# Row-wise softmax of a batched diagonal: half batches in row-by-row dot products against whole batches in wide products and sums

## The chip, the cores and the metric

The kernel runs on one core of a Trainium2 chip. The metric is the device time of one execution in microseconds (us), the median of several runs. Profiled executions give the details; their own time stands beside their span, which is the time from the first to the last of the program's instructions.

The engines that matter here are VectorE (DVE in the profile), which does the dot products, ScalarE (ACT), which does the exponentials and issues the output transfers, GpSimd (POOL), which reduces across partitions, and SyncE (SP), which only issues the input transfers. 16 DMA engines move the data.

## The reference

`x` and `y` are float32 of shape (8, 4096, 512). Of the product of x and the transposed y only the diagonal is needed, so each of the 8 x 4096 outputs begins as the dot product of one row of x with the same row of y:

```python
gram = np.matmul(x, y.transpose(0, 2, 1))
diag = np.diagonal(gram, axis1=1, axis2=2)
diag = diag - diag.max(axis=-1, keepdims=True)
exp = np.exp(diag)
return (exp / exp.sum(axis=-1, keepdims=True)).astype(np.float32)
```

The softmax runs over the 4096 values of a batch. Each input is read once, 134.22 MB in all; the output has 0.13 MB.

## The kernel before

A batch has 4096 rows. They are laid over 128 partitions, so that partition p holds rows 32p to 32p + 31, which is one run of 64 KB in memory. A batch is worked on in two halves of 16 rows to a partition (`H = 16`).

The loop at L82 goes over batches and halves. For each half, `load` (L38) takes a new x tile and a new y tile from a pool with three buffers for each, and issues one transfer for each of the two on SP's queue, 4 MB apiece, in which each partition gets one run of 32 KB (L43, L44). The last half of the last batch is cut into pieces of 8, 4, 2, 1 and 1 rows. A load into a buffer that was used before waits until the dot products that read it are done; that wait stands on SP, and the transfers behind it on SP wait too.

`dots` (L48) then runs one VectorE instruction for each of the 16 rows (L51): it multiplies 512 elements of x and y, writes the products over x, and leaves their sum in one column of `diag`. The sum comes out of an accumulator, which shows in the profile as a second instruction, a read of the accumulator.

After the second half, `softmax` (L61) takes the maximum of the 32 columns (L65), the maximum over the partitions on GpSimd (L67), its negative (L69), the exponentials with their sums on ScalarE (L71), the sum over the partitions on GpSimd (L76), the reciprocal (L78) and the scaling (L79), and sends 128 runs of 128 bytes to the output from ScalarE's queue (L80).

The framework puts the semaphores for all this. Transfers from SP and ScalarE share eight completion semaphores in turn, so a transfer also waits until the transfer that had its semaphore before has landed.

Of the kernel before, what the change touches and what calls it, by code (L numbers as in the profile page):

```python
# [1 line left out]

# [5 lines left out]


@with_exitstack
def kernel(
    ctx: ExitStack,
    tc: tile.TileContext,
    x: bass.AP,
    y: bass.AP,
    out: bass.AP,
):
    nc = tc.nc
    f32 = mybir.dt.float32  # L20
    B, N, D = x.shape
    P = nc.NUM_PARTITIONS
    R = N // P
    H = R // 2


    xv = x.rearrange("b (p r) d -> b p r d", p=P)
    yv = y.rearrange("b (p r) d -> b p r d", p=P)
    ov = out.rearrange("b (p r) -> b p r", p=P)

    io = ctx.enter_context(tc.tile_pool(name="io", bufs=3))
    persist = ctx.enter_context(tc.tile_pool(name="persist", bufs=1))
    sm = ctx.enter_context(tc.tile_pool(name="sm", bufs=2))

    diag = persist.tile([P, B * R], f32, name="diag")
    res = persist.tile([P, B * R], f32, name="res")

    def load(b, r0, parts):  # L38
        xt = io.tile([P, H, D], f32, tag="xt", name="xt")
        yt = io.tile([P, H, D], f32, tag="yt", name="yt")  # L40
        o = 0
        for n in parts:
            nc.sync.dma_start(out=xt[:, o : o + n, :], in_=xv[b, :, r0 + o : r0 + o + n, :])  # L43
            nc.sync.dma_start(out=yt[:, o : o + n, :], in_=yv[b, :, r0 + o : r0 + o + n, :])  # L44
            o += n
        return xt, yt

    def dots(b, r0, xt, yt):  # L48
        for k in range(H):
            c = b * R + r0 + k  # L50
            nc.vector.scalar_tensor_tensor(  # L51
                out=xt[:, k, :],
                in0=xt[:, k, :],
                scalar=1.0,
                in1=yt[:, k, :],
                op0=mybir.AluOpType.mult,
                op1=mybir.AluOpType.mult,
                accum_out=diag[:, c : c + 1],
            )

    def softmax(b):  # L61
        db = diag[:, b * R : (b + 1) * R]
        rb = res[:, b * R : (b + 1) * R]
        mxp = sm.tile([P, 1], f32, tag="mxp", name="mxp")
        nc.vector.tensor_reduce(out=mxp, in_=db, axis=mybir.AxisListType.X, op=mybir.AluOpType.max)  # L65
        mx = sm.tile([P, 1], f32, tag="mx", name="mx")
        nc.gpsimd.partition_all_reduce(out_ap=mx, in_ap=mxp, channels=P, reduce_op=bass_isa.ReduceOp.max)  # L67
        nmx = sm.tile([P, 1], f32, tag="nmx", name="nmx")
        nc.vector.tensor_single_scalar(out=nmx, in_=mx, scalar=-1.0, op=mybir.AluOpType.mult)  # L69
        sump = sm.tile([P, 1], f32, tag="sump", name="sump")  # L70
        nc.scalar.activation(  # L71
            out=rb, in_=db, func=mybir.ActivationFunctionType.Exp,
            bias=nmx, scale=1.0, accum_out=sump,
        )
        ssum = sm.tile([P, 1], f32, tag="ssum", name="ssum")
        nc.gpsimd.partition_all_reduce(out_ap=ssum, in_ap=sump, channels=P, reduce_op=bass_isa.ReduceOp.add)  # L76
        rc = sm.tile([P, 1], f32, tag="rc", name="rc")
        nc.vector.reciprocal(out=rc, in_=ssum)  # L78
        nc.vector.tensor_single_scalar(out=rb, in_=rb, scalar=rc, op=mybir.AluOpType.mult)  # L79
        nc.scalar.dma_start(out=ov[b], in_=rb)  # L80

    for b in range(B):  # L82
        for h in range(2):
            last = b == B - 1 and h == 1
            parts = [8, 4, 2, 1, 1] if last else [H]
            xt, yt = load(b, h * H, parts)
            dots(b, h * H, xt, yt)
        softmax(b)


# [1 line left out]
_INS = ['x', 'y']  # L92
_OUTS = [((8, 4096), 'float32')]


# [23 lines left out]
```

## Time and profile before

| | before |
|---|---|
| median of 10 runs | 325.54 us (325.39 to 325.71) |
| the profiled execution's own time | 325.62 us |
| its span | 323.8 us |
| VectorE busy | 164.3 us, 544 instructions |
| ScalarE busy, GpSimd busy | 4.6 us, 6.1 us |
| input transfers (queue q1) | 5760 packets, 134.22 MB, 96.6% of 16 engines' time |
| output transfers (queue q10) | 1152 packets, 0.13 MB, 0.3% |
| mean rate of all transfers over the span | 415 GB/s |

Busy time is the time in which an engine has an instruction under way; issuing a transfer and waiting do not count. The share of a DMA queue is the time that its packets took, over the span of 16 engines. In the groups of instructions, the time after the bar is the busy time and the mean of one instruction in nanoseconds, then the time that the engine was idle just before, and what ended that. Instruction counts of the profile leave out waits. Since the instructions of one row overlap, a row takes less time than one instruction lasts: 16 rows take 9.90 us in the chain of waits, 0.62 us a row, where the instruction lasts 687 ns.

### The profile page before, as it was taken

The numbers are of one execution on the slowest core, as the hardware profiler recorded it, in microseconds if no ns is written. First come the engines' busy times: TensorE is split into PE (matmuls) and PEld (weight loads), VectorE is DVE, ScalarE is ACT, GpSimd is POOL, SyncE is SP. The second block draws the span as 40 slices with busy tenths as digits, with TensorE's granted clock in tenths as the row PEclk, the third lists the DMA queues.
The fourth block names the chain that finished last, engine by engine and source line by source line (L and its number), as shares of the span: only waits on it lengthen the run. The fifth ranks groups of instructions, "written<-read, shape, count | busy, mean of one in ns | idle before, by whom it ended". The sixth has DMA issues, their size and how long they took to land.

```text
span 323.8 us, 727 instructions
## 1 busy us (share of the span) xinstructions
DVE 164.3 (51%) x544; ACT 4.6 (1%) x17; POOL 6.1 (2%) x20
## 2 busy tenths in 40 slices
DVE  0029084290944709256191742908348091571994
ACT  1000000000000000000000000000000000000000
POOL 0000000000000000000000000000000000000000
DMA  8999999999999999999999999999999999999980
GB/s 324 453 405 437 453 426 413 455 421 421 453 429 415 454 421 418 454 419 425 453 421 421 456 413 429 449 414 434 449 413 433 450 403 441 449 409 427 417 313 10
DMA packets 6917, 134.39 MB, mean 415 GB/s; under 512 B 1792, under 2 KB 1792, under 8 KB 2560
## 3 DMA queue, kind: packets, MB, share of 16 engines
q1 hardware_dynamic: 5760, 134.22, 96.6%
q10 hardware_dynamic: 1152, 0.13, 0.3%
q14 instruction: 5, 0.04, 0.0%
HBM read 134.22 MB, written 0.13 MB: 415 GB/s over the span
## 4 chain that ended last, share of the span: by engine, by line
DMA 82%; DVE 16%; issue 1%; SPq 0%; POOLq 0%; POOL 0%; DVEq 0%
DMA yt<-in_y_dram 82%; DVE xt L51 16%; SPq L43 0%; DVE mxp L65 0%; POOLq L114 0%; POOL mx L67 0%; DVE res L79 0%; DVE rc L78 0%; DVEq L51 0%; DVEq L79 0%; POOLq L67 0%
## 5 line engine op out<-in xcount | busy, mean ns | idle before, releaser
L51 DVE SCALAR_TENSOR_TENSOR xt<-xt,yt 128x512 f32<-128x512 f32 x256 | 158.2, 687 | 144.2 <-DMA yt<-in_y_dram 144.1
L51 DVE DVE_READ_ACCUMULATOR xt<-xt,yt 128x1 f32 x256 | 21.1, 82 | 0.0
L67 POOL PARTITION_ALL_REDUCE mx<-mxp x8 | 2.8, 350 | 308.9 <-DVE mxp L65 308.9
L71 ACT ACTIVATE res<-diag,nmx 128x32 f32<-128x32 f32 x8 | 2.6, 321 | 315.2 <-DVE nmx L69 315.2
L78 DVE RECIPROCAL rc<-ssum 128x1 f32<-128x1 f32 x8 | 1.3, 164 | 7.6 <-POOL ssum L76 7.6
L69 DVE TENSOR_SCALAR nmx<-mx 128x1 f32<-128x1 f32 x8 | 1.2, 154 | 4.3 <-POOL mx L67 4.3
L76 POOL PARTITION_ALL_REDUCE ssum<-sump x8 | 3.1, 383 | 5.8 <-ACT res L71 5.8
L79 DVE TENSOR_SCALAR res<-res,rc 128x32 f32<-128x32 f32 x8 | 1.9, 241 | 0.9
L65 DVE TENSOR_REDUCE mxp<-diag 128x1 f32<-128x32 f32 x8 | 1.5, 186 | 0.3
L71 ACT ACTIVATION_READ_ACCUMULATOR res<-diag,nmx 128x1 f32 x8 | 1.5, 187 | 0.0
L71 ACT ACT_TABLE_LOAD x1 | 1.3, 1283 | 0.7 <-PEq L103 0.7
L103 POOL MEMSET const-float32-0.0<- 128x1 f32 x1 | 0.1, 98 | 0.2 <-issue 0.2
L103 POOL MEMSET const-bfloat16-1.0<- 128x1 bf16 x1 | 0.1, 102 | 0.0
L103 POOL MEMSET const-uint8-127<- 128x1 uint8 x1 | 0.1, 101 | 0.0
L103 POOL MEMSET const-float32-1.0<- 128x1 f32 x1 | 0.1, 98 | 0.0
## 6 DMA issues: line engine op xcount, KB each, us to landing
xt<-in_x_dram SPq DMA_DIRECT2D x15, 4096.0 KB, 39.6
yt<-in_y_dram SPq DMA_DIRECT2D x15, 4096.0 KB, 48.9
xt<-in_x_dram SPq DMA_DIRECT2D x1, 2048.0 KB, 34.8
yt<-in_y_dram SPq DMA_DIRECT2D x1, 2048.0 KB, 39.3
xt<-in_x_dram SPq DMA_DIRECT2D x1, 1024.0 KB, 41.3
yt<-in_y_dram SPq DMA_DIRECT2D x1, 1024.0 KB, 43.3
xt<-in_x_dram SPq DMA_DIRECT2D x1, 512.0 KB, 35.5
yt<-in_y_dram SPq DMA_DIRECT2D x1, 512.0 KB, 27.0
```

The source lines that it names most:

```text
L51: nc.vector.scalar_tensor_tensor(out=xt[:, k, :], in0=xt[:, k, :], scalar=1.0, in1=yt[:, k, :], op0=mybir.AluOpType.mult, op1=mybir.AluOpT ...
L65: nc.vector.tensor_reduce(out=mxp, in_=db, axis=mybir.AxisListType.X, op=mybir.AluOpType.max)
L67: nc.gpsimd.partition_all_reduce(out_ap=mx, in_ap=mxp, channels=P, reduce_op=bass_isa.ReduceOp.max)
L69: nc.vector.tensor_single_scalar(out=nmx, in_=mx, scalar=-1.0, op=mybir.AluOpType.mult)
L71: nc.scalar.activation(out=rb, in_=db, func=mybir.ActivationFunctionType.Exp, bias=nmx, scale=1.0, accum_out=sump,)
L76: nc.gpsimd.partition_all_reduce(out_ap=ssum, in_ap=sump, channels=P, reduce_op=bass_isa.ReduceOp.add)
L78: nc.vector.reciprocal(out=rc, in_=ssum)
L79: nc.vector.tensor_single_scalar(out=rb, in_=rb, scalar=rc, op=mybir.AluOpType.mult)
L103: nc = _bacc.Bacc("TRN2", target_bir_lowering=False, num_devices=1)
```

## The change

The kernel is laid out anew, with the order of its instructions as written.

There are now two whole x tiles, `xs0` and `xs1`, used in turn, and a single y tile, `ys`. Each has 32 rows to a partition, 64 KB.

Batches 0 to 5 are loaded with one transfer for x and one for y, each of 8 MB. One VectorE instruction multiplies all 32 rows, 16384 elements to a partition, over x (`dots_wide`), and a second one sums them in 32 groups of 512 (`sums_wide`). The next load into `ys` waits for the product; the next load into the same x tile waits for the sums.

Batch 6 is loaded with one transfer for x and two halves for y, and its dot products run row by row as before. Batch 7 comes in pieces of 8, 8, 8, 4, 2, 1 and 1 rows, also row by row. Each of its y pieces goes into `ys` and so waits for those rows of batch 6 that lie there.

The softmax runs in three groups. Batches 0 to 4 are done together (`group_exp` after the sums of batch 4, `group_out` between the product and the sums of batch 5); batches 5 and 6 together, with `group_exp` before row 2 of batch 7 and `group_out` before its row 10; batch 7 alone, by the same instructions as before (`last_softmax`). In the groups, the negative and the scaling are on ScalarE, and each group has one output transfer, with runs of 128 bytes.

```diff
-    io = ctx.enter_context(tc.tile_pool(name="io", bufs=3))
...
+    ctx.enter_context(tc.manual_schedule())
...
+    xs = [big.tile([P, R, D], f32, name=f"xs{i}") for i in range(2)]
+    ys = big.tile([P, R, D], f32, name="ys")
...
+    def load_x(b, r0, n):
+        nc.sync.dma_start(out=xs[b % 2][:, r0 : r0 + n, :], in_=xv[b, :, r0 : r0 + n, :])
+
+    def load_y(b, r0, n):
+        nc.sync.dma_start(out=ys[:, r0 : r0 + n, :], in_=yv[b, :, r0 : r0 + n, :])
+
+    def dots_wide(b):
+        xt = xs[b % 2]
+        nc.vector.tensor_tensor(out=xt, in0=xt, in1=ys, op=Alu.mult)
+
+    def sums_wide(b):
+        nc.vector.tensor_reduce(out=diag[:, b, :], in_=xs[b % 2], axis=X, op=Alu.add)
+
+    def dot_row(b, r):
+        xt = xs[b % 2]
+        nc.vector.scalar_tensor_tensor(
+            out=xt[:, r, :],
+            in0=xt[:, r, :],
+            scalar=1.0,
+            in1=ys[:, r, :],
+            op0=Alu.mult,
+            op1=Alu.mult,
+            accum_out=diag[:, b, r : r + 1],
+        )
+
+    def group_exp(name, b0, n):
...
+        nc.vector.tensor_reduce(out=mxp, in_=diag[:, b0 : b0 + n, :], axis=X, op=Alu.max)
+        nc.gpsimd.partition_all_reduce(out_ap=mx, in_ap=mxp, channels=P, reduce_op=bass_isa.ReduceOp.max)
+        nc.scalar.mul(nmx, mx, -1.0)
+        for i in range(n):
+            nc.scalar.activation(
+                out=res[:, b0 + i, :], in_=diag[:, b0 + i, :], func=Act.Exp,
+                bias=nmx[:, i : i + 1], scale=1.0, accum_out=sump[:, i : i + 1],
             )
+        nc.gpsimd.partition_all_reduce(out_ap=ssum, in_ap=sump, channels=P, reduce_op=bass_isa.ReduceOp.add)
+        return ssum
...
+    def group_out(name, b0, n, ssum):
+        rc = column(name + "rc", n)
+        nc.vector.reciprocal(out=rc, in_=ssum)
+        for i in range(n):
+            rb = res[:, b0 + i, :]
+            nc.scalar.activation(out=rb, in_=rb, func=Act.Copy, scale=rc[:, i : i + 1])
+        nc.scalar.dma_start(out=ov[:, b0 : b0 + n, :], in_=res[:, b0 : b0 + n, :])
...
-    for b in range(B):
-        for h in range(2):
-            last = b == B - 1 and h == 1
-            parts = [8, 4, 2, 1, 1] if last else [H]
-            xt, yt = load(b, h * H, parts)
-            dots(b, h * H, xt, yt)
-        softmax(b)
+    for b in range(wide):
+        load_x(b, 0, R)
+        load_y(b, 0, R)
+        dots_wide(b)
+        if b == wide - 1:
+            group_out("a", 0, wide - 1, first)
+        sums_wide(b)
+        if b == wide - 2:
+            first = group_exp("a", 0, wide - 1)
+
+    b = B - 2
+    load_x(b, 0, R)
+    for r0 in (0, R // 2):
+        load_y(b, r0, R // 2)
+        for r in range(r0, r0 + R // 2):
+            dot_row(b, r)
+
+    b = B - 1
+    r0 = 0
+    for n in (8, 8, 8, 4, 2, 1, 1):
+        load_x(b, r0, n)
+        load_y(b, r0, n)
+        for r in range(r0, r0 + n):
+            if r == 2:
+                second = group_exp("b", B - 3, 2)
+            if r == 10:
+                group_out("b", B - 3, 2, second)
+            dot_row(b, r)
+        r0 += n
+    last_softmax(b)
```

Here `B` is 8, `R` is 32 and `wide` is 6.

More of the change, by code (lines that the diff above doesn't have):

```diff
@@ L19 @@
     nc = tc.nc
+    ctx.enter_context(tc.manual_schedule())
     f32 = mybir.dt.float32
+    Alu = mybir.AluOpType
+    Act = mybir.ActivationFunctionType
+    X = mybir.AxisListType.X
     B, N, D = x.shape
@@ L23 @@
     R = N // P
-    H = R // 2
+    wide = B - 2
     xv = x.rearrange("b (p r) d -> b p r d", p=P)
     yv = y.rearrange("b (p r) d -> b p r d", p=P)
-    ov = out.rearrange("b (p r) -> b p r", p=P)
-    io = ctx.enter_context(tc.tile_pool(name="io", bufs=3))
[L32 to L58, printed above, removed]
-            )
@@ L61, in softmax @@
[L61 to L75, printed above, removed]
+    ov = out.rearrange("b (p r) -> p b r", p=P)
@@ new lines, with column @@
+    big = ctx.enter_context(tc.tile_pool(name="big", bufs=1))
+    small = ctx.enter_context(tc.tile_pool(name="small", bufs=1))
+    xs = [big.tile([P, R, D], f32, name=f"xs{i}") for i in range(2)]
+    ys = big.tile([P, R, D], f32, name="ys")
+    diag = small.tile([P, B, R], f32, name="diag")
+    res = small.tile([P, B, R], f32, name="res")
+    def column(name, n):
+        return small.tile([P, n], f32, name=name)
+    def load_x(b, r0, n):
+        nc.sync.dma_start(out=xs[b % 2][:, r0 : r0 + n, :], in_=xv[b, :, r0 : r0 + n, :])
@@ new lines, in group_exp @@
+    def group_exp(name, b0, n):
+        mxp, mx, nmx, sump, ssum = (column(name + s, n) for s in ("mxp", "mx", "nmx", "sump", "ssum"))
+        nc.vector.tensor_reduce(out=mxp, in_=diag[:, b0 : b0 + n, :], axis=X, op=Alu.max)
[5 more added lines that the diff above has]
+                bias=nmx[:, i : i + 1], scale=1.0, accum_out=sump[:, i : i + 1],
+            )
+        nc.gpsimd.partition_all_reduce(out_ap=ssum, in_ap=sump, channels=P, reduce_op=bass_isa.ReduceOp.add)
+        return ssum
@@ new lines, in group_out, with last_softmax @@
+    def group_out(name, b0, n, ssum):
[5 more added lines that the diff above has]
+        nc.scalar.dma_start(out=ov[:, b0 : b0 + n, :], in_=res[:, b0 : b0 + n, :])
+    def last_softmax(b):
+        db, rb = diag[:, b, :], res[:, b, :]
+        mxp, mx, nmx, sump, ssum, rc = (column("l" + s, 1) for s in ("mxp", "mx", "nmx", "sump", "ssum", "rc"))
+        nc.vector.tensor_reduce(out=mxp, in_=db, axis=X, op=Alu.max)
+        nc.gpsimd.partition_all_reduce(out_ap=mx, in_ap=mxp, channels=P, reduce_op=bass_isa.ReduceOp.max)
+        nc.vector.tensor_single_scalar(out=nmx, in_=mx, scalar=-1.0, op=Alu.mult)
+        nc.scalar.activation(out=rb, in_=db, func=Act.Exp, bias=nmx, scale=1.0, accum_out=sump)
@@ L76, in softmax @@
         nc.gpsimd.partition_all_reduce(out_ap=ssum, in_ap=sump, channels=P, reduce_op=bass_isa.ReduceOp.add)
-        rc = sm.tile([P, 1], f32, tag="rc", name="rc")
         nc.vector.reciprocal(out=rc, in_=ssum)
-        nc.vector.tensor_single_scalar(out=rb, in_=rb, scalar=rc, op=mybir.AluOpType.mult)
-        nc.scalar.dma_start(out=ov[b], in_=rb)
-    for b in range(B):
-        for h in range(2):
-            last = b == B - 1 and h == 1
-            parts = [8, 4, 2, 1, 1] if last else [H]
-            xt, yt = load(b, h * H, parts)
-            dots(b, h * H, xt, yt)
-        softmax(b)
+        nc.vector.tensor_single_scalar(out=rb, in_=rb, scalar=rc, op=Alu.mult)
@@ new lines, in last_softmax @@
+        nc.scalar.dma_start(out=ov[:, b, :], in_=rb)
+    for b in range(wide):
[14 more added lines that the diff above has]
+    b = B - 1
```

## The prediction

> **What bounds the kernel now.** I read the table of DMA queues first, then the chain that ended last, then a table of stretches, then the timeline at both ends. The columns of the queue table are packets, MB, and the share of 16 DMA engines' time.
>
> ```profile
> DVE 164.3 (51%) x544; ACT 4.6 (1%) x17; POOL 6.1 (2%) x20
> q1 hardware_dynamic: 5760, 134.22, 96.6%
> q14 instruction: 5, 0.04, 0.0%
> by line: DMA yt<-in_y_dram 81.9%; DVE xt L51 15.5%; issue 0.6%; SPq L43 0.5%; DVE mxp L65 0.2%; POOLq L114 0.1%; POOL mx L67 0.1%; DVE res L79 0.1%; DVE rc L78 0.1%; DVEq L51 0.0%; DVEq L79 0.0%; POOLq L67 0.0%
> L51 DVE SCALAR_TENSOR_TENSOR xt<-xt,yt 128x512 f32<-128x512 f32 x256 | 158.2, 687 | 144.2 <-DMA yt<-in_y_dram 144.1
> SPq L43 <- DVE xt L51: 133.0, 7, 19.7
> ```
>
> VectorE works half the time and idles 144 us, nearly all of it for y. SP waits up to 19.7 us for free buffers (last line), so its queue is always fed. The loads set the time, and VectorE's share in the chain is only that releases pass through it. The stretches (length, busy VectorE, ScalarE, GpSimd, clock, DMA share, GB/s) tell more:
>
> ```profile
> 22.47:61.20 38.73, 20.52 (x68) 0.41 (x2) 0.73 (x2) 1.00 1.00 433
> 303.40:314.60 11.20, 11.20 (x39) 0.00 (x0) 0.00 (x0) 1.00 0.94 377
> 314.60:318.40 3.80, 3.23 (x11) 0.00 (x0) 0.00 (x0) 1.00 0.06 22
> 318.40:323.80 5.40, 1.45 (x6) 0.41 (x2) 0.73 (x2) 1.00 0.03 5
> ```
>
> The first row is the full rate, 433 GB/s. The third is the surprise: for 3.8 us the DMA share is 0.06, one engine of sixteen. Fifteen engines are done by 314.6 and one works alone until 318.4. The last row is the tail, softmax and output, 5.4 us.
>
> The trace's packet records say why one engine is late. At 47.4, 124.9, 185.5 and 263.0 us an 8,192-byte packet of the instruction queue (q14) takes 0.31 to 0.33 us, and the 32 KB packet that starts just after it takes 1.87 us against 1.21: together 0.97 us lost each time. In the landing times of the 16 engines, the last lags the fifteenth by 0.1 us before the first fetch, then by 0.9, 1.8, 2.9 and 3.9. When the fetches start, VectorE has begun 53, 191, 306 and 444 instructions (waits included), about 130 apart; no other engine runs so many. I conclude that they are VectorE's instruction stream, and that the last 3.9 us of the load stage are these four fetches.
>
> **What the Trainium skill says.** (1) "Runtime: NRT & Kernel Launch", section Instruction fetch mechanics: the sequencer fetches its instructions by its own DMA queue, 256 in a 16 KiB block, thus 64 bytes each. The trace agrees in kind, its block is 8 KiB, which is 128 instructions and close to the 130 above. (2) "DMA: Bandwidth & Descriptors", section Where 436 GB/s comes from: a ceiling of 435 GB/s; the 433 here is nearly that, so transfers in bulk can gain very little. (3) "VectorE: DVE Perf Modes", section on the TRN2 errata: an fp32 product of two tensors takes (N+151)/0.96 ns. For N = 512 that is 691, the row above has 687. (4) The same page's perf-mode tier table has tensor_reduce at one element a cycle; the trace's 128x32 reduce at 186 ns fits 32 cycles with that fixed part.
>
> **The change, part by part.** The model is per DMA engine, and I check it on the kernel before. A packet of 16 KB takes 611 ns and one of 32 KB 1213, so a packet costs 9 ns beside its bytes.
>
> *Packets.* Each transfer has 128 runs, 8 on an engine, and one completion packet of 9 ns. Before: 40 transfers, 320 packets an engine. After: 12 whole-batch loads, x and two halves of y for batch 6, and 14 pieces of batch 7 make 29 transfers, 232 packets. Gain: 88 x 9 + 11 x 9 ns = 0.9 us. No trace shows a 64 KB run. If it is cut in two, the wide part has 104 packets more and the gain is gone (bounds 0 and 0.9 us). I take one packet.
>
> *Instruction fetches.* VectorE's 544 counted instructions become 148: 6 products, 6 sums, 2 group maxima and 2 reciprocals, 64 rows with 64 accumulator reads, 4 in the last softmax; with waits some 166 to 170. The first fetch came at the 53rd, the next at the 191st. So one fetch is left, at about row 12 to 15 of batch 6, near 278 us. Three of four go: 3 x 0.97 = 2.9 us off the late engine. Bounds: none left, 3.9; none removed, 0. I take 2.9.
>
> *The wide products and the new wait.* The product of 32 rows has N = 16384: 17.22 us as an estimate from (3). Below it stands 16384/0.96 = 17.07, above it 32 rows at their pace of 0.613 us, 19.6. There is one ys, so the issue of y(b+1) on SP waits for the product of batch b, and x(b+2) and all later loads stand behind it. Meanwhile x(b+1) flows. How long does a queue take to restart? At the start of the span:
>
> ```profile
> 0.72 0.36 SPq L43 DMA_DIRECT2D xt<-in_x_dram  x1
> 1.13 21.33 DMA yt<-in_y_dram
> ```
>
> x is issued at 0.72 and y, two transfers of 9.71 us later, has landed at 22.46, so 2.3 us are latency on idle engines. The loop from y to y is 0.09 (landing to VectorE) + 17.22 + 0.03 (to SP) + 2.3 + 19.35 (the y load at one packet per 64 KB) = 39.0 us; the loads of a batch alone are 38.7. So the gap g at each of y1 to y5 and the first half of y6 is at most 0.3 us at the cold latency. It is less if the reads of y overlap the end of x: the descriptors arrive 1.0 us after the issue (first packet at 1.72), and x has then 1.0 us to go. The last output shows a short way too, 1.4 us from issue to landing. I take g = 0.05, 6 x 0.05 = 0.3 us; bounds 0 and 2.0.
>
> *Sums.* x(b+2) waits for the sums of b: 17.2 + 17.2 after y(b) landed, issue 34.5 after it, and the queue is full until 38.7. Cover 4.2 us less a latency of 2.3; each us beyond that costs 5 us in all. Nothing charged. The first group's maximum (0.2) and the reciprocal sit in the same slack.
>
> *Rows of batches 6 and 7.* The sums of batch 5 end near 269.3; the 32 rows of batch 6 end at 289. Pieces of y7 wait for the rows of batch 6 in ys: rows 0 to 7 are done at 274.3, while y6 lands until 273.4 and the first x7 piece covers until 278.3. Later pieces have 5 us or more. VectorE has caught up before piece three (lands near 302.8), so the last row starts at its landing, as before.
>
> *Outputs.* The second group's output takes up the completion semaphore that the first group's output used, and the last x piece is the next user, so its issue on SP waits for that output. Output packets alternate with load packets on each engine (before, 8 of them took 13.5 us beside 32 KB packets). 40 packets of the first group from 254.8 pass by about 289; the second output is issued near 296.5 and its 16 pass by 306. The last x piece must be out by 309.5. Cover 3.5 us, nothing charged; beyond that every us costs one.
>
> *Tail.* The last softmax has the same instructions: 5.48 us from the last landing (318.36) to the span's end.
>
> Sum: the fifteenth engine's last landing, 314.63, less 0.9 = 313.7; one fetch +0.97 = 314.7; gaps +0.3 = 315.0; tail +5.48 = 320.5 span. The profiled execution took 325.62 with a span of 323.84, 1.78 around it: 322.3. The median is 0.08 below that execution: **322.2 us**.
>
> **Rivals.** *The gap opens* (slower). If product and latency together are longer than 19.2 (19.35 less the 0.12 of handing over), each batch adds the excess as g. At 321.9 without gaps, g = 0.7 brings it beyond 326.2, so it decides at product plus latency of 19.9. With the row pace as the product, 19.6, and the cold latency, g = 2.7 and 16 us are lost: 338. I price it half way, g = 1.35: 330. For it: one buffer for y and only 1 us between arrival of descriptors and dry queues. Against it: the formula fits the 687 ns row. *The late engine stays late* (no change): the fetches are not VectorE's, or another delay takes the engine; only packets are gained, 322.2 + 2.9 = 325.1. For it: the fetches are unevenly spaced (138, 115, 138 instructions). *Small gain*: g = 0.3 six times and 64 KB runs cut in two, 322.2 + 1.7 + 0.9 = 324.8. *Larger gain*: no fetch at all and no gap, 320.9.
>
> **How the numbers follow.** Main case 0.67, with the larger gain 0.70 (320.9 to 324); small gain 0.07; no change 0.10; slower 0.13. A change under about 0.2% (0.65 us) cannot be told from none. Faster 0.77, same 0.10, slower 0.13. The range, 320.9 to 325.3, leaves out the slower case and little more.
>
> **What would show it.** Right: y(b) landings 38.7 to 39.0 us apart; one q14 packet besides the start's and the end's, after 240 us; one engine alone for about 1 us at the end instead of 3.8; products near 17.2 us; q1 with 29 x 144 = 4,176 packets. Wrong: products over 18 us, a DMA share clearly under 1.00 at the end of each x, SP waiting for the second output, or again four fetches.

## The result: 332.6 us, 2.1% slower

| | before | after |
|---|---|---|
| median | 325.59 us (31 runs, 325.39 to 325.75) | 332.6 us (9 runs, 330.35 to 333.79) |
| ratio to before | | 1.0208 (95% interval 1.0195 to 1.0221) |
| profiled execution, its span | 325.62, 323.8 us | 332.23, 330.5 us |
| last landing of an input | 318.36 us | 325.01 us |
| last landing to the span's end | 5.48 us | 5.44 us |

The forecast was 322.2 us. The runs after also scatter by 3.4 us, where those of before scatter by 0.4.

These are the engine lines, the DMA queues and the groups of the page of the kernel after:

```profile
DVE 247.6 (75%) x148; ACT 6.2 (2%) x26; POOL 3.3 (1%) x10
q1 hardware_dynamic: 4176, 134.22, 95.6%
q14 instruction: 1, 0.01, 0.0%
DMA 58%; DVE 39%; issue 2%; SPq 0%; POOLq 0%; ACT 0%; POOL 0%; DVEq 0%; ACTq 0%
L55 DVE TENSOR_TENSOR xs<-xs,ys 128x16384 f32<-128x16384 f32 x6 | 103.3, 17225 | 71.6 <-DMA ys<-in_y_dram 71.6
L58 DVE TENSOR_REDUCE diag<-xs 128x32 f32<-128x16384 f32 x6 | 103.3, 17220 | 0.2
```

The counts are as forecast: 148 VectorE instructions, 4,176 packets, a single fetch of instructions (at 286.5 us in the packet records), products of 17.2 us. But VectorE's share of the chain has gone from 16% to 39%: the product is now a link between one load of y and the next. This is the chain in order of time (start, length, what):

```profile
1.14 40.91 DMA ys<-in_y_dram
...
42.16 17.24 DVE xs L55
59.39 0.02 issue
59.41 23.72 DMA ys<-in_y_dram
...
83.22 17.24 DVE xs L55
100.46 0.02 issue
100.48 22.23 DMA ys<-in_y_dram
...
140.05 23.61 DMA ys<-in_y_dram
...
181.01 23.88 DMA ys<-in_y_dram
...
222.24 21.98 DMA ys<-in_y_dram
```

Each y row runs from its issue to its landing. The data of one such load takes 19.35 us (8 packets of 2.418 us on each engine), so 4.4, 2.9, 4.3, 4.5 and 2.6 us go by beside the data. For 2.0 to 2.2 us of that the load stands behind the end of x, and nothing is lost; the rest is a hole. The landings of y are therefore 41.1, 39.6, 41.0, 41.2 and 39.3 us apart, against the 38.7 us that the bytes of a batch need.

In the stretches (length, busy VectorE, ScalarE, GpSimd, clock, DMA share, GB/s) the hole is directly visible behind the first such issue:

```profile
42.06:59.41 17.35, 17.23 (x1) 0.00 (x0) 0.00 (x0) 1.00 0.98 423
59.41:63.00 3.59, 3.58 (x1) 0.00 (x0) 0.00 (x0) 1.00 0.89 292
42.06:244.22 202.16, 172.55 (x11) 1.84 (x11) 0.84 (x2) 1.00 0.98 415
275.14:322.00 46.86, 40.37 (x122) 1.45 (x7) 1.53 (x2) 1.00 1.00 421
```

A packet counts with its bytes where it starts, so a short stretch shows a rate only roughly; the long third one is solid: 415 GB/s instead of 433. In the fourth, where y comes in small pieces and several transfers are always queued, the DMA share is 1.00 again. The packet records give the detail. After the issue at 59.41 the engines end x between 60.5 and 61.1. Most start y between 60.8 and 61.3, but two only at 61.97 and 62.69. The first y packet takes 2.9 to 3.65 us instead of 2.42, as the first packets at the start of the kernel do (2.6 to 3.5).

### The profile page after: what moved, and what is told of

It is laid out like the page before. It is cut to its first block, busy times and chain, and to the rows that moved or that the text cites. A ratio compares the mean times of both kernels' runs of the same rounds, so it can differ in the third digit from the quotient of the medians.

```text
span 330.5 us, 298 instructions
## 1 busy us (share of the span) xinstructions
DVE 247.6 (75%) x148; ACT 6.2 (2%) x26; POOL 3.3 (1%) x10
## 3 DMA queue, kind: packets, MB, share of 16 engines
q1 hardware_dynamic: 4176, 134.22, 95.6%
## 4 chain that ended last, share of the span: by engine, by line
DMA 58%; DVE 39%; issue 2%; SPq 0%; POOLq 0%; ACT 0%; POOL 0%; DVEq 0%; ACTq 0%
DMA ys<-in_y_dram 54%; DVE xs L55 31%; DVE diag L58 4%; DVE xs L62 4%; DMA out_dram<-res 3%; SPq L48 0%; POOLq L161 0%; ACT res L91 0%; POOL lmx L98 0%; DVE res L103 0%; DVE lmxp L97 0%; DVE lrc L102 0%; DVEq L55 0%; DVE arc L88 0%; DVE brc L88 0%
## 5 line engine op out<-in xcount | busy, mean ns | idle before, releaser
L55 DVE TENSOR_TENSOR xs<-xs,ys 128x16384 f32<-128x16384 f32 x6 | 103.3, 17225 | 71.6 <-DMA ys<-in_y_dram 71.6
L58 DVE TENSOR_REDUCE diag<-xs 128x32 f32<-128x16384 f32 x6 | 103.3, 17220 | 0.2
L62 DVE SCALAR_TENSOR_TENSOR xs<-xs,ys 128x512 f32<-128x512 f32 x64 | 39.8, 689 | 7.2 <-DMA ys<-in_y_dram 7.1
L62 DVE DVE_READ_ACCUMULATOR xs<-xs,ys 128x1 f32 x64 | 5.4, 84 | 0.0
L79 ACT ACTIVATE res<-diag,anmx 128x32 f32<-128x32 f32 x5 | 1.5, 308 | 0.0
L91 ACT ACTIVATE res<-res,arc 128x32 f32<-128x32 f32 x5 | 1.2, 309 | 19.5 <-DVE arc L88 19.5
L76 POOL PARTITION_ALL_REDUCE bmx<-bmxp x1 | 0.7, 735 | 57.1 <-DVE bmxp L75 57.1
L79 ACT ACTIVATION_READ_ACCUMULATOR res<-diag,anmx 128x1 f32 x5 | 0.9, 187 | 0.0
L83 POOL PARTITION_ALL_REDUCE bssum<-bsump x1 | 0.8, 800 | 1.1 <-ACT res L79 1.1
```

What stands on the lines that cost most here:

```text
L55: nc.vector.tensor_tensor(out=xt, in0=xt, in1=ys, op=Alu.mult)
L58: nc.vector.tensor_reduce(out=diag[:, b, :], in_=xs[b % 2], axis=X, op=Alu.add)
L62: nc.vector.scalar_tensor_tensor(out=xt[:, r, :], in0=xt[:, r, :], scalar=1.0, in1=ys[:, r, :], op0=Alu.mult, op1=Alu.mult, accum_out=diag ...
L79: nc.scalar.activation(out=res[:, b0 + i, :], in_=diag[:, b0 + i, :], func=Act.Exp, bias=nmx[:, i : i + 1], scale=1.0, accum_out=sump[:, i ...
L91: nc.scalar.activation(out=rb, in_=rb, func=Act.Copy, scale=rc[:, i : i + 1])
```

## Experiments

All times are medians; the kernel before, run beside them, took 325.48 us in the first group of four and 325.56 us in the second.

| run | what differs | us | ratio to before (95% interval) |
|---|---|---|---|
| e1_runs32 | changed kernel, runs of 32 KB | 333.55 | 1.0246 (1.0194 to 1.0298) |
| e2_yhalves | changed kernel, y and product in halves | 322.53 | 0.9909 (0.9894 to 0.9924) |
| e3_prod28 | changed kernel, product of 28 rows | 322.18 | 0.9909 (0.9889 to 0.9930) |
| e8_prod30 | changed kernel, product of 30 rows | 328.01 | 1.0070 (1.0045 to 1.0096) |
| e5_prod36 | changed kernel, 4 rows multiplied twice | 338.79 | 1.0410 (1.0394 to 1.0425) |
| e6_wide_before | kernel before, wide products and sums | 322.90 | 0.9911 (0.9895 to 0.9928) |
| e7_more_instr | kernel before, 512 more instructions | 329.31 | 1.0110 (1.0095 to 1.0125) |
| e9_all32 | e2 with runs of 32 KB | 323.27 | 0.9924 (0.9909 to 0.9939) |

Two theories stood at first. In theory 1 the queue of loads runs dry at each y. In theory 2 the runs of 64 KB, whose packets hold an engine for 2.4 us, are the trouble. What is still to be transferred when a load is issued is called its cover below.

### Shorter runs, same wait

```diff
-        load_x(b, 0, R)
-        load_y(b, 0, R)
+        load_x(b, 0, R // 2)
+        load_x(b, R // 2, R // 2)
+        load_y(b, 0, R // 2)
+        load_y(b, R // 2, R // 2)
         dots_wide(b)
```

> The changed kernel, but in batches 0 to 5 each load of x and of y is cut into two transfers with runs of 32 KB; the product of 32 rows stays whole, so both halves of y still wait for it. Theory 1 (the queue runs dry: y is issued 2.0 us before the end of x, and a restart among running transfers takes 2.1 us on the median engine and up to 4.5 us on the last): the wait is unchanged, so the time stays near the 332.6 us of the changed kernel, plus about 1.0 us for 96 more packets and 12 more completions on each engine, 332 to 334, and the landings of y stay some 40.4 us apart. Theory 2 (runs of 64 KB hold the engines up and make the descriptors late): the gaps shrink or go, 323 to 326 us, landings 38.9 us apart.

It took 333.55 us (331.19 to 335.71; the profiled execution is the fastest of them). The landings of whole batches of y are at 41.9, 82.6, 122.0, 161.6, 203.2 and 243.8 us, 40.4 apart. Theory 2 falls: with runs of 32 KB and the same wait, the gaps are the same. The engine that is served last is as late as with long runs (it lands up to 2.6 us after the first).

### y and the product in halves

```diff
-        nc.vector.tensor_tensor(out=xt, in0=xt, in1=ys, op=Alu.mult)
+        for r in (0, R // 2):
+            xh, yh = xt[:, r : r + R // 2, :], ys[:, r : r + R // 2, :]
+            nc.vector.tensor_tensor(out=xh, in0=xh, in1=yh, op=Alu.mult)
...
-        load_y(b, 0, R)
+        load_y(b, 0, R // 2)
+        load_y(b, R // 2, R // 2)
```

> The changed kernel, but in batches 0 to 5 the y load and the product are each done in two halves of 16 rows; x stays one transfer of 64 KB runs. The first half of the next y can then be issued 8.6 us after the product began, with 10 us of x still to come. Theory 1 (dry queue): all gaps go; 322.2 us of the prediction less its 0.3 for gaps plus 0.5 for 48 more packets and 6 completions, about 322.4 us, landings of whole batches 38.8 us apart. Theory 2 (64 KB runs): x still has them, so at least half of the loss of 10 us stays, 327 us or more.

It took 322.53 us (322.44 to 322.61), faster than both kernels, with x still in runs of 64 KB. The chain of this variant:

```profile
32.26 8.70 DVE xs L57
40.96 0.02 issue
40.98 29.95 DMA ys<-in_y_dram
...
71.02 8.70 DVE xs L57
79.72 0.02 issue
79.74 29.96 DMA ys<-in_y_dram
```

and its stretch from the first whole y to the last of batch 5:

```profile
41.87:235.76 193.89, 173.33 (x16) 1.84 (x11) 0.85 (x2) 1.00 1.00 433
```

The first half of the next y is issued at 40.98, even before the second half of this y has landed (41.87), with all of the next x between them. That is more cover than the expectation said, since the half product need not wait for the whole y. From issue to landing it now takes 29.95 us, which is time in the queue and costs nothing: 433 GB/s, five batches in 193.89 us, 38.8 each.

### Moving the moment of the issue

The product of 28 rows and of 30 rows brings the issue forward, four rows multiplied twice put it off. The first two leave y out of four and of two rows of each wide batch, the third multiplies four rows by y once too often; none of them computes the softmax of the reference. They are there for their times only.

```diff
-        nc.vector.tensor_tensor(out=xt, in0=xt, in1=ys, op=Alu.mult)
+        nc.vector.tensor_tensor(out=xt[:, 0:28, :], in0=xt[:, 0:28, :], in1=ys[:, 0:28, :], op=Alu.mult)
```

> The changed kernel, but the wide product takes only 28 of the 32 rows of a batch (the other four are summed without y, so that part of the computation is left out). The product is shorter by 2048/0.96 ns = 2.13 us, and y is issued that much earlier, with 4.1 us of x left. Theory 1 (dry queue): the median engine no longer runs dry and only engines that are served last lose something, up to 0.4 us a batch: 322 to 325 us. Theory 2 (64 KB runs): nothing changes, 332 us.

> The changed kernel with a wide product of 30 of the 32 rows (two rows of each batch are summed without y). y is issued 1.07 us earlier than in the changed kernel, with 3.1 us of x left. If a restart took only the 2.3 us seen on idle engines, nothing would be lost: 322 us. If the engine that is served last takes up to 4.5 us when the others still run, batches lose between 0 and 1.4 us: 323 to 329 us, and its runs scatter by more than 1 us.

```diff
         nc.vector.tensor_tensor(out=xt, in0=xt, in1=ys, op=Alu.mult)
+        nc.vector.tensor_tensor(out=xt[:, 0:4, :], in0=xt[:, 0:4, :], in1=ys[:, 0:4, :], op=Alu.mult)
```

> The changed kernel with one more VectorE instruction after each wide product, which multiplies four of its rows a second time (so those sums are not the reference's). y is issued about 2.2 us later. Theory 1 (dry queue): each of six restarts is later by the full 2.2 us, 332.6 + 13 = 345 to 347 us. Theory 2 (64 KB runs): VectorE has some 6 us of idle time in each batch, so the time stays near 332.6 us.

| | x still to come at the issue of y | time | gap in each of 6 places (time less 321.9, over 6) |
|---|---|---|---|
| 28 rows | 4.1 us | 322.18 | 0.05 us |
| 30 rows | 3.1 us | 328.01 | 1.0 us |
| 32 rows (the change) | 2.0 us | 332.6 | 1.8 us |
| 32 + 4 rows | -0.3 us | 338.79 | 2.8 us |

321.9 us is the sum of the prediction without gaps. The moment of the issue alone moves the time by 16.6 us, as theory 1 has it, but not by theory 1's amount on the late side: I expected 345 to 347 us and got 338.8. The chain of that run says why:

```profile
59.35 2.30 DVE xs L56
61.66 0.02 issue
61.67 21.85 DMA ys<-in_y_dram
...
100.88 2.30 DVE xs L56
103.18 0.02 issue
103.19 21.90 DMA ys<-in_y_dram
...
144.76 21.86 DMA ys<-in_y_dram
```

Here x has wholly landed (61.33) before y is issued, and the restart takes 21.9 - 19.35 = 2.5 us every time: all sixteen engines start between 62.62 and 63.09. That is close to the 2.3 us read at the start of the kernel before, and to the 2.6 us at the start of this run, whose packets have 64 KB (x issued at 0.72, landed at 22.66). These runs scatter by 0.2 us. With 30 rows, y is issued while x still runs, with 3.1 us to go. At a latency of 2.3 us it would stand behind x for 3.1 us and lose nothing. But (this is the fastest of its seven runs, 326.57 us):

```profile
58.18 23.17 DMA ys<-in_y_dram
...
97.63 24.55 DMA ys<-in_y_dram
...
138.46 23.61 DMA ys<-in_y_dram
...
178.35 22.53 DMA ys<-in_y_dram
```

Less the 19.35 us of data, these are 3.8, 5.2, 4.3 and 3.2 us to the landing on the last engine, up to 2.1 us more than the wait behind x. In the second of them the eighth engine has landed at 119.86 and the two last ones at 122.1. With 28 rows all but one of nine runs lie between 322.0 and 322.5 us, and one took 325.08. So about 4 us of cover is where the gaps nearly end here.

### The instruction fetches

In the kernel before, only the form of the dot products was changed, in batches 0 to 6:

```diff
+    def dots_wide(b, r0, xt, yt):
+        c = b * R + r0
+        nc.vector.tensor_tensor(out=xt, in0=xt, in1=yt, op=mybir.AluOpType.mult)
+        nc.vector.tensor_reduce(out=diag[:, c : c + H], in_=xt, axis=mybir.AxisListType.X, op=mybir.AluOpType.add)
...
-            dots(b, h * H, xt, yt)
+            (dots if b == B - 1 else dots_wide)(b, h * H, xt, yt)
```

> The kernel before with its tiles, transfers and waits as they are; only in batches 0 to 6 the 16 rows of a half are one wide product and one wide sum, so that VectorE has some 165 instructions instead of 575 (waits included). Theory of the fetches (one 8 KB packet of instructions for every 128 instructions or so of VectorE, 0.97 us each on one and the same DMA engine): one fetch is left of four, the last engine ends about 1 us after the others, 325.5 - 2.9 = 322.6 us. Rival (the fetches belong to something else, or the late engine is late anyway): four fetches and 325.5 us.

It took 322.90 us (322.69 to 323.04), one fetch of instructions (at 240.9 us). The reverse, two more instructions written behind each row:

```diff
                 accum_out=diag[:, c : c + 1],
             )
+            nc.vector.memset(spare, 0.0)
+            nc.vector.memset(spare, 0.0)
```

> The kernel before with two VectorE instructions that write zero to one spare column after each row, 512 more instructions of under 0.1 us; 16 rows then take some 12 us of the 19.4 between landings, so VectorE stays hidden. Theory of the fetches: four more, eight in all, 325.5 + 3.9 = 329.4 us, plus up to 0.2 for the last rows. Rival (VectorE's instruction count doesn't matter): 325.5 to 325.8 us and four fetches.

It took 329.31 us (329.22 to 329.33). The added instructions did not stay behind their rows: the framework moved them forward, and all 512 ran between 0.8 and 107.4 us. The packet records show eight fetches during the loads and one after them; the page counts all nine, against one for the wide form:

```profile
DVE 193.8 (59%) x1056; ACT 4.6 (1%) x17; POOL 6.1 (2%) x20
q14 instruction: 9, 0.07, 0.1%
```

Five of the eight fetches come at 9.8, 27.6, 50.4, 72.1 and 93.7 us, while the added instructions run, the other three at 128.7, 189.3 and 266.8 us. From one to the next VectorE has begun 110 to 138 instructions (waits included), as in the kernel before. In its stretch behind the landing of the fifteenth engine, one engine works alone for 7.3 us, where the kernel before had 3.7:

```profile
314.70:322.00 7.30, 6.86 (x23) 0.00 (x0) 0.00 (x0) 1.00 0.06 24
```

The landing times agree: the last engine is 7.4 us after the fifteenth with eight fetches, 3.7 with four, 0.7 with one. From run to run that is 0.9 to 1.0 us a fetch in both directions, and the fetches follow VectorE's instruction count.

The wide form in the kernel before gains as much (0.9911) as the variant of the changed kernel with y in halves (0.9909). These runs resolve no gain from the new tiles, the longer runs and the grouped softmax beside that of the fewer instructions.

### What the long runs are worth

```diff
-        load_x(b, 0, R)
+        load_x(b, 0, R // 2)
         load_y(b, 0, R // 2)
+        load_x(b, R // 2, R // 2)
         load_y(b, R // 2, R // 2)
```

> The variant with y and the product in halves, but x in halves too, so that all runs of batches 0 to 5 are 32 KB. No queue runs dry in either. The packet model of 9 ns a packet says 48 more packets and 6 more completions on each engine, 0.5 us: 322.5 + 0.5 = 323.0 us. If 64 KB runs are of no use, 322.5; if they hold anything up, less than 322.5 us.

It took 323.27 us (322.92 to 323.51) against 322.53 of the variant with long x runs, in another group of runs; by the ratios to before, 0.9924 and 0.9909, the difference is 0.5 us, but their intervals overlap. It fits the packet model (5,904 packets against 5,040) and doesn't prove it. The two profiled executions agree with it too: from the landing of the first whole y to that of batch 5, runs of 32 KB take 194.28 us where long x runs took 193.89. The packet records show the rest: a 64 KB run is one packet of 2.418 us, 8 ns less than two of 1.213.

## Why the prediction was wrong

- **Packets: right.** 4,176 on q1, and one packet for a run of 64 KB. 0.9 us was taken for it; its time alone wasn't resolved.
- **Instruction fetches: right**, in number in this kernel (one for four) and in size in the two experiments built for it. The one at 286.5 us cost 0.84 us, 0.31 for itself and 0.53 in the 16 KB packet behind it. They are most of what the variant with halves gains: its 322.53 us is close to the prediction's sum without gaps plus its smaller packets, 322.4.
- **Products and sums: right.** 17.23 and 17.22 us. The estimate of 17.22 came from the formula that the Trainium skill gives for an fp32 addition of two tensors ("VectorE: DVE Perf Modes", the section on the TRN2 errata); here the product and the sum keep to it. x(b+2) was never late because of the sums.
- **The restart: wrong, and nearly the whole error.** The step that failed is the term of 2.3 us in the loop from y to y, 0.09 + 17.22 + 0.03 + 2.3 + 19.35 = 39.0 us, with its conclusion that g is at most 0.3 us, and 0.05 if reads overlap. The loop is the right one; the term of 2.3 us, taken from idle engines, came out at 2.6 to 4.5 us among running transfers, 3.7 in the mean. I had called the idle value an upper bound, and reasoned that descriptors that arrive while x still runs can only help. They didn't: less the data's 19.35 us, the eighth engine landed 2.1 to 2.6 us after the issue, against 2.1 to 2.2 with the queue empty (32 + 4 rows). And a load lands when its last engine does, which was later still. Even the 2.5 us of an empty queue would have made g 0.5 us, some 3 us in all (an estimate from the loop); the rest is the late engines. The 5 restarts cost 202.16 - 5 x 38.75 = 8.4 us beyond the forecast of 38.7 + 0.05 a batch. The first half of batch 6's y landed 30.92 us after the last wide y, where 19.35 + 9.71 = 29.06 were due, another 1.9. Together that is 10.3 us, where the measured last landing (325.01) is 10.0 behind the predicted one (315.0).
- **The rival that the gap opens** named the place and the price per us: it was to decide at a product plus latency of 19.9 us, and 17.2 + 3.7 (the mean of the five restarts) = 20.9 is beyond it. But I let it hang on a slow product, which the formula spoke against, and so gave it 0.13. That its price of 330 us came near the measured time is chance: it stood for a slow product, and the restart was what was slow.
- **The small-gain rival** was summed 0.2 us too high: 322.2 has 0.3 us of gaps already, so six gaps of 0.3 add 1.5 and not 1.7. Nothing hangs on it.
- **The outputs: right that they cost nothing.** Beside packets of load the second output took 10.4 us from issue to landing, and the last x piece was issued at its landing, 317.59. The pieces before it were still landing until 323.75 (on the first engine until 321.83), and the last landings stay 0.63 us apart, so nothing was lost. But the cover was nearer 2 us than the 3.5 forecast: the last x piece came out 7.4 us before the last landing, where the prediction needed 5.5 (309.5 to 315.0).
- **The tail: right**, 5.44 us for 5.48.

Why a few engines are served late when a load is issued into running transfers isn't settled. Run size is excluded by the first experiment. The records name no engine, so it couldn't be seen which of the sixteen they are, nor whether they are always the same.

## What to carry to other kernels

A transfer that waited for its buffer needed more cover here than its latency on an idle machine: measure what remains in the queue at the moment of the issue, and compare it with the slowest engine's restart (here up to 5.2 us; with 4.1 us in the queue the gaps were nearly gone), not with the first load of the kernel. Splitting such a buffer so that its first part can be refilled early cost a few packets and took the loss of the gaps away here. When transfers bound a kernel, look whether one DMA engine finishes late, and count the other packets that it carries: here instructions, nearly 1 us for each 8 KB. Fewer and wider instructions gained 2.7 us here (325.56 to 322.90), though VectorE had time to spare.

## What the runs showed of the hardware that I had not expected

- A load issued just before the queue runs dry reached its last engine later after its issue than one issued into an empty queue: less the time of its data, up to 4.5 us with 2.0 us of transfers ahead of it and up to 5.2 us with 3.1 us, against some 2.5 us every time. Counted from the start of the product, the earlier issue was still the better one.
- One 8 KB packet of VectorE's instructions came for about every 128 of them, on one and the same DMA engine (its lag adds up from fetch to fetch), and cost it 0.97 us: 0.3 for itself and 0.65 in the 32 KB packet behind it. "Runtime: NRT & Kernel Launch", section Instruction fetch mechanics, in the Trainium skill says that fetches are hidden by the pace of the instructions. For VectorE that holds here (its rows follow one another at 0.61 us through the fetch at 47.4 us of the kernel before); for the loads that share the DMA engine it doesn't.
- The first packets behind the hole at 59.41 us took 0.5 to 1.2 us longer than their bytes need, and those into an empty queue (32 + 4 rows) 0.2 to 1.1 us. With 28 rows, at the first three issues of y, none took over 0.1 us longer. So a restart can be recognised in these packet records.
